# Value sums ordered behind the newest one-hots, the dense picks as a background task, score tiles in other PSUM banks and row norms one head later, in an encoder layer with expert retrieval

## The chip, the cores and the metric

One core of a Trainium2 chip. The metric is the device time of one execution in microseconds. Before the change three runs gave a median of 1346.87 us (1346.04 to 1347.17). The engines are PE (TensorE), DVE (VectorE), ACT (ScalarE), POOL (GpSimd) and SP (SyncE, which here only issues transfers). Every engine works off its own list of instructions in order.

## The reference

One encoder layer is applied to two sequences of 256 tokens, width 1024, each with 16 learned meta tokens in front: the *prompt* (s = 0) and the *sample* (s = 1). After a mixer (short gated convolution beside grouped-query attention) comes a retrieval over 128 x 128 = 16384 experts:

```python
q = (xf @ wq).reshape(T, 8, 2, 128)                  # 8 heads, two halves
s = einsum('thpc,hpnc->thpn', q, subkeys)            # 128 key scores per half
sv, si = top_k(s, 16)                                # 16 keys of each half
cv, cp = top_k(all 256 sums of the two halves, 16)   # 16 of the pairs
eidx = expert numbers;  gates = softmax(cv)
a = gelu(einsum('thkd,td->thk', u_tab[eidx], x)) * gates
out = einsum('thk,thkd->td', a, v_tab[eidx])         # 128 experts per token
```

Everything is float32.

## The kernel before, in words

**Two ways through the experts.** The prompt's experts are fetched: its 2 x 128 tokens have 128 experts each, and one transfer (`g_issue`, L178, on POOL's queue) brings for one rank `k` the rows `u` and `v` of the chosen expert of 128 tokens, 128 x 8 KB = 1.0486 MB, into a tile `grow`. There are 256 such transfers and four buffers for them. For each, DVE forms the dot product with the token (`g_dot`, L208, tile `grow`, result into `dots`), ACT applies gelu and the gate to `dots` (`g_weight`, L200 and L202), and DVE adds the weighted `v` row to the output row `xh` (`g_val`, L191: the *value sum*). Only then is the buffer free for the next transfer. The sample's experts are computed densely: scores of all 16384 experts in 128 *score blocks* `j` (a 512 KB load `u`, then matmuls `pSj`, L136, which the profile records 16 times a block), four blocks to a PSUM tile, evacuated with gelu by `experts` into `Al` and `Ah`; gates for all experts, mostly zero; and values in 128 blocks (`acc`, L1046) over 64 loads `v` of 1 MB. Every third value block is split into a high and a low part (`vhl`, `ah`, `al`).

**The order of the stages** in the trace: mixer of the prompt to 134 us, its retrieval projections to 190, mixer of the sample to 334, its projections (`projections`, matmuls `pqq`, key scores `pn`, L383) to 404, scores to 914, values to the end.

**The gates.** `gates_dense` runs beside the scores. After the picks are finished (`fin1`) it makes, in 64 steps of four tokens, one-hot tiles `oi` and `oj` on DVE, weighted copies `gh` and `gl` of `oj` on ACT, and products `pgm` on PE (`gate_products`, L919 and L920); every second step the products are copied into `Al` and `Ah` (ACT, blocks whose scores are not yet out) or multiplied into them (DVE, the others). Its small tiles lie in the pool `og`, which is closed when it ends; the first `v` tiles are then laid in that space.

**What paces the background.** Inside the loops `bg(us)` is called with the PE time of the piece just written, 3.5 for a score block, and pays two accounts: `credit["a"]` by `share["a"]`, of which each gather step costs `GU` = 2.65, and `credit["b"]` by `share["b"]`, of which the tasks (generators that yield their cost) are paid. Without a task `a` gets the sum of both shares, at most `SMAX`. In the stage of the sample's projections `step1` makes the picks of a head at once, inside the loop, and puts gather steps between them by `SR`. From block 3 on the shares are `SS` = 0.72 and `SBS` = 0.42. What is left of the 256 transfers at the values stage is spread over its blocks by `want`, each transfer waiting for the matmul of its block (`pe_mark`).

**Who sets the order.** The program writes instructions in the order of the Python code, and the tile framework's scheduler then reorders them on each engine within their dependencies. `order(i, before)` ties an instruction behind another of the same engine in that order, with no wait of its own. Before, each dot and each value sum is tied to the newest DVE instruction written at that moment (L190 to L192, L207 to L210).

**The row norms.** The sample's tokens `xr` enter the projections unscaled. `rescale` (L868) makes, at head 0, a PSUM tile `pb` of the row norms (`pb`, L877), and DVE multiplies it into the eight chunks of `xr` (L881); the key scores of the head projected before that are scaled in their evacuation (`hp < 2`).

**PSUM at the scores.** `psS`, two tiles of two banks for the scores, is opened before `psg`, two tiles for key scores and gate products; `acc` later takes the space of `psg`.

Of the kernel before, what the change touches and what calls it, by code (L numbers as in the profile page):

```python
# [37 lines left out]
SR = 0.6  # L38
SS = 0.72
SMAX = 0.74  # L40
SPL = 3
SBS = 0.42
# [3 lines left out]
def encoder_layer(ctx: ExitStack, tc: tile.TileContext, xp, xs_, meta, vec, w_in, w_out, wq,  # L46
# [23 lines left out]
    act = Recorded(nc.scalar, last_act)  # L70

# [3 lines left out]
    def ps(name, bufs):  # L75
        return tc.tile_pool(name=name, bufs=bufs, space=PSUM, reuse_waits="tile")
# [35 lines left out]
    def weights(src, s, split=False):  # L112

        w = [wtile("w").rearrange("p (c n) -> p c n", c=4) for _ in range(2)]
        for q in range(2):
            nc.sync.dma_start(w[q], src[:, s, 4 * q:4 * q + 4])
        if not split:
            return lambda c, k=0: w[c // 4][:, c % 4]
        k = 1 + 2 * spl[0]
        spl[0] = 1 - spl[0]  # L120
        hl = [ga[k + i].tile([P, 2 * D], F32R, tag="g", name=n).rearrange("p (q x) -> p q x", q=2)
              for i, n in enumerate(("whi", "wlo"))]
        for q in range(2):
            f = w[q].rearrange("p c n -> p (c n)")
            act.activation(hl[0][:, q], f, AF.Copy)
            dve.tensor_tensor(hl[1][:, q], f, hl[0][:, q].bitcast(F32), op=ALU.subtract)
        v = [x.rearrange("p q (c n) -> p (q c) n", c=4) for x in hl]
        return lambda c, k=0: v[k][:, c]
# [54 lines left out]
    def order(i, before):  # L183
        tc.add_manual_dep(i.ins, before.ins.name,
                          mybir.DependencyInfo(mybir.DependencyClass.NoSync, mybir.DependencyReason.DATA),
                          reason="order")

    def g_val():
        t, k, r = vals.pop(0)
        before = last[0]  # L190
        i = dve.scalar_tensor_tensor(gctx["h"], r[:, D:], dots[:, k:k + 1], gctx["h"], op0=ALU.mult, op1=ALU.add)  # L191
        order(i, before)  # L192
        if t == 0 and k == P - 1:
            pool.dma_start(yp[0:P, :], gctx["h"])
            gctx["h"] = gctx["next"][1]
# [19 lines left out]
    direct = [False]  # L215

# [158 lines left out]
    def projections(xr, sk, scores, qp, step=None, split=False, rescale=None, lag=1):  # L375
# [4 lines left out]
        def key_scores(hp, qs, pl=None, tag="tr"):  # L380
# [3 lines left out]
            if hp < 2 and rn is not None:  # L384
                for t in range(2):
                    act.activation(scores[:, hp, t], pn[:, t], AF.Copy, scale=rn[:, t:t + 1])
            else:
                act.activation(scores[:, hp], pn, AF.Copy)
# [3 lines left out]
        for hd in range(PH):  # L392
            w = weights(wq, hd, split)
            for pp in range(2):
# [7 lines left out]
                if hd == 0 and rescale is not None:  # L402
                    rn = rescale(xr, pp)
# [25 lines left out]
    w_kv = weights(w_in, 0, True)  # L429
# [39 lines left out]
    def front(s, h, rn):  # L469
# [17 lines left out]
        for t in range(2):  # L487
# [5 lines left out]
            if sp:  # L493
                dve.tensor_scalar_mul(x, h[:, t, :], stat)
            else:
                act.activation(x, h[:, t, :], AF.Copy, scale=stat)
# [363 lines left out]
    def step1(hd):  # L860
        share["a"] = 0.0
        for us in heads1(hd, [0, 1]):
            more(us * SR)
        topk_left[0] -= 1
# [3 lines left out]
    def rescale(xr, pp):  # L868

        if pp == 0:  # L870
# [13 lines left out]
    share.update(a=SR, b=0.0)  # L884
# [3 lines left out]
    psS = ctx.enter_context(ps("psS", 2))  # L888
    psgx = ExitStack()
    psg = psgx.enter_context(ps("psg", 2))  # L890
    r_done = [0]
    tau = [0]

    def gates_dense():
# [5 lines left out]
        yield 6.0  # L900
# [35 lines left out]
        for t in range(2):  # L936
# [15 lines left out]
            yield 3.0  # L952
            for o in range(P // OC):
# [7 lines left out]
                dve.tensor_tensor(v4(oi), sl4(0), ib, op=ALU.is_equal)  # L961
# [7 lines left out]
                if o == 0:  # L969
                    yield 2.0  # L970
                yield 1.3 + (4 * r_done[0] + 60) / 700
# [18 lines left out]
    for j in range(P):  # L990
# [12 lines left out]
        if j == 3:  # L1003
            tasks.append(gates_dense())
            share.update(a=SS, b=SBS)
# [124 lines left out]
```

## Time and profile before

| | us |
|---|---|
| median of 3 runs | 1346.87 |
| the profiled execution | 1346.99 |
| its span in the trace | 1345.2 |
| PE busy | 1275.6 (95%) |
| DVE busy | 1056.0 (78%) |
| transferred | 459.68 MB, mean 342 GB/s |
| value sums, 256 on DVE | 1282 ns each |
| dots, 256 on DVE | 1221 ns each |
| one-hots, `oi` or `oj` | 420 ns each |

The profiled execution lies 1.8 us above its span (what is outside of the first and last instruction). An idle time in the trace's timeline stands in brackets with what ended it. The granted clock is the share of full speed that TensorE had in a stretch. A DMA busy share of 1.00 means that all 16 DMA engines were busy throughout.

### The profile page before, as it was taken

The numbers are of one execution on the slowest core, as the hardware profiler recorded it, in microseconds if no ns is written. First come the engines' busy times: TensorE is split into PE (matmuls) and PEld (weight loads), VectorE is DVE, ScalarE is ACT, GpSimd is POOL, SyncE is SP. The second block draws the span as 40 slices with busy tenths as digits, with TensorE's granted clock in tenths as the row PEclk, the third lists the DMA queues.
The fourth block names the chain that finished last, engine by engine and source line by source line (L and its number), as shares of the span: only waits on it lengthen the run. The fifth ranks groups of instructions, "written<-read, shape, count | busy, mean of one in ns | idle before, by whom it ended". The sixth has DMA issues, their size and how long they took to land.

```text
span 1345.2 us, 17868 instructions
## 1 busy us (share of the span) xinstructions
PE 1275.6 (95%) x6038; PEld 965.0 (72%) x6038; DVE 1056.0 (78%) x2279; ACT 549.9 (41%) x1621; POOL 389.1 (29%) x480
## 2 busy tenths in 40 slices
PE   6999998998898999969999999996999999999998
PEld 5888996777787887758888888884555555555554
DVE  5656998885799998679888787897677777777767
ACT  5555641742221311148776555663222222222221
POOL 1111223431223343543233232231222232222221
PEclk9999998998999999989999999997999999999999
DMA  5534636658998999999999999997999999999997
GB/s 174 160 108 152 214 106 219 216 192 317 365 333 309 383 417 415 416 412 386 399 396 399 397 415 354 409 403 275 410 420 422 421 420 415 420 420 418 415 422 324
DMA packets 80859, 459.68 MB, mean 342 GB/s; under 512 B 9456, under 2 KB 9968, under 8 KB 39552
## 3 DMA queue, kind: packets, MB, share of 16 engines
q0 software_dynamic: 37296, 270.02, 50.1%
q1 hardware_dynamic: 42032, 183.57, 35.9%
q10 hardware_dynamic: 1440, 4.95, 1.0%
q8 instruction: 47, 0.77, 0.2%
q14 instruction: 44, 0.36, 0.1%
HBM read 454.28 MB, written 4.19 MB: 341 GB/s over the span
## 4 chain that ended last, share of the span: by engine, by line
PE 37%; DMA 17%; DVE 7%; issue 3%; ACT 2%; POOL 0%; DVEq 0%; POOLq 0%; ACTq 0%; SPq 0%
PE acc L1046 27%; DMA grow<-in_uv,eidx 16%; PE pSj L136 9%; DVE xh L63 3%; DVE grow L63 2%; DMA v<-in_v_n 1%; DVE Ah L63 1%; ACT dots L63 1%; DVE Al L63 1%; PE pgm L920 1%; PE pgm L919 1%; ACT gh L63 0%; ACT pSj L63 0%; DVE vhl L63 0%; ACT gl L63 0%
## 5 line engine op out<-in xcount | busy, mean ns | idle before, releaser
L178 POOL DMA_INDIRECT grow<-in_uv,eidx x256 | 317.2, 1239 | 717.2 <-DVE xh L63 233.5
L136 PE MATMUL pSj<-xr,u 128*128 128x256 f32 x2048 | 468.9, 386 | 7.4 <-ACT Ah L63 4.7
L136 PEld LDWEIGHTS pSj<-xr,u 128*128 128x128 f32 x2048 | 386.2, 192 | 69.0 <-DMA u<-in_u_t 7.5
L63 DVE SCALAR_TENSOR_TENSOR xh<-grow,dots,xh 128x1024 f32<-128x1024 f32 x256 | 328.2, 1282 | 58.4 <-ACT dots L63 57.2
L63 DVE SCALAR_TENSOR_TENSOR grow<-grow,xh 128x1024 f32<-128x1024 f32 x256 | 312.5, 1221 | 70.2 <-DMA grow<-in_uv,eidx 69.2
L63 ACT ACTIVATE dots<-dots 128x1 f32<-128x1 f32 x256 | 51.7, 202 | 544.8 <-DVE grow L63 544.4
L1046 PE MATMUL acc<-v,Al 128*128 128x512 f32 x496 | 220.1, 597 | 5.1 <-DMA v<-in_v_n 5.1
L1046 PEld LDWEIGHTS acc<-v,Al 128*128 128x128 f32 x496 | 94.9, 191 | 113.0 <-issue 110.5
L1046 PE MATMUL acc<-vhl,ah 128*128 128x512 f32 x336 | 107.4, 441 | 0.0
L63 ACT ACTIVATE gh<-oj,ghi 128x128 f16<-128x128 f16 x256 | 99.5, 389 | 6.2 <-PE pgm L919 5.7
L63 ACT ACTIVATE gl<-oj,glo 128x128 f16<-128x128 f16 x256 | 99.5, 389 | 0.0
L63 DVE TENSOR_TENSOR vhl<-v,vhl 128x1024 fp32r<-128x1024 f32 x42 | 51.4, 1224 | 55.6 <-ACT vhl L63 55.6
L1046 PEld LDWEIGHTS acc<-vhl,ah 128*128 128x128 f32 x336 | 63.2, 188 | 30.2 <-issue 19.1
L1046 PE MATMUL acc<-v,Ah 128*128 128x512 f32 x192 | 84.3, 592 | 0.0
L63 ACT ACTIVATE dots<-dots,gate_all 128x1 f32<-128x1 f32 x256 | 74.6, 292 | 7.0
L63 DVE TENSOR_TENSOR wlo<-w,whi 128x1024 fp32r<-128x1024 f32 x42 | 51.1, 1218 | 19.6 <-ACT whi L63 13.4
L1046 PEld LDWEIGHTS acc<-v,Ah 128*128 128x128 f32 x192 | 36.4, 190 | 41.2 <-issue 40.2
L136 PE MATMUL pqq<-xr,w 128*128 128x256 f32 x256 | 60.0, 388 | 0.8 <-DMA w<-in_wq 0.8
L136 PEld LDWEIGHTS pqq<-xr,w 128*128 128x128 f32 x256 | 48.6, 195 | 8.1 <-DMA w<-in_wq 1.4
L919 PE MATMUL pgm<-gh,oi 128*128 128x128 f16 x256 | 36.8, 222 | 16.1 <-DVE oi L63 15.1
L63 ACT ACTIVATE vhl<-v 128x1024 fp32r<-128x1024 f32 x42 | 44.0, 1048 | 19.1 <-DMA v<-in_v_n 18.4
L63 ACT ACTIVATE whi<-w 128x1024 fp32r<-128x1024 f32 x42 | 43.9, 1058 | 18.3 <-PE pqq L136 8.5
(279 smaller groups left out, 1753.6 us busy)
## 6 DMA issues: line engine op xcount, KB each, us to landing
u<-in_u_t SPq DMA_DIRECT2D x128, 512.0 KB, 8.6
v<-in_v_n SPq DMA_DIRECT2D x64, 1024.0 KB, 8.9
w<-in_w_in SPq DMA_DIRECT2D x36, 512.0 KB, 3.9
w<-in_wq SPq DMA_DIRECT2D x32, 512.0 KB, 6.1
w<-in_w_out SPq DMA_DIRECT2D x16, 512.0 KB, 4.7
grow<-in_uv,eidx POOLq DMA_INDIRECT x256, 10.1
hdram<-h ACTq DMA_DIRECT2D x3, 512.0 KB, 2.7
h<-in_xp SPq DMA_DIRECT2D x2, 512.0 KB, 5.9
```

Source lines behind the costliest of these rows:

```text
L63: i = f(*a, **k)
L136: i = pe.matmul(out, st_(c, a), mv(c, b), start=(n == 0), stop=(n == NC * len(terms) - 1))
L178: i = pool.indirect_dma_start(out=r, out_offset=None, in_=uv, in_offset=bass.IndirectOffsetOnAxis(ap=eidx[:, t, k:k + 1], axis=0))
L919: pe.matmul(pg[:, q, :], oi[:, r, :], gh[:, r, :], start=True, stop=False)
L920: pe.matmul(pg[:, q, :], oi[:, r, :], gl[:, r, :], start=False, stop=True)
L1046: i = pe.matmul(acc[t][q], a[:, t * P:(t + 1) * P], v[:, q * 512:(q + 1) * 512], start=j == 0 and n == 0, stop=j == P - 1 and n == len(ter ...
```

## The change

The picks of the sample become a background task, paid by `SRB` = 0.58 in the projections (`SR` is 0.57 instead of 0.6); the shares of the scores' stage, now `SSG` = 0.75 and `SBS` = 0.46, are set when the first one-hots are due and no longer at block 3, and `SMAX` goes from 0.74 to 0.66. A value sum is tied behind the newest `oi`. The row norms are multiplied into `xr` after the second head, so key scores of two heads are scaled in their evacuation. `psg` is opened before `psS`. The first weights' low parts (`wlo`) are ordered behind the first normalized tile (`xs`).

```diff
-SR = 0.6
-SS = 0.72
-SMAX = 0.74
+SR = 0.57
+SRB = 0.58
+SSG = 0.75
+SMAX = 0.66
-SBS = 0.42
+SBS = 0.46
...
+        def convert(behind=None):
+            for q in range(2):
+                f = w[q].rearrange("p c n -> p (c n)")
+                act.activation(hl[0][:, q], f, AF.Copy)
+                i = dve.tensor_tensor(hl[1][:, q], f, hl[0][:, q].bitcast(F32), op=ALU.subtract)
+                if behind is not None:
+                    order(i, behind)
...
         order(i, before)
+        if last_oi[0] is not None:
+            order(i, last_oi[0])
...
-            if hp < 2 and rn is not None:
+            if hp < 4 and rn is not None:
...
-                if hd == 0 and rescale is not None:
-                    rn = rescale(xr, pp)
+                if hd < 2 and pp and rescale is not None:
+                    rn = rescale(xr, hd)
...
-    w_kv = weights(w_in, 0, True)
+    convert_kv, w_kv = weights(w_in, 0, True, True)
...
-                dve.tensor_scalar_mul(x, h[:, t, :], stat)
+                i = dve.tensor_scalar_mul(x, h[:, t, :], stat)
+                if t == 0:
+                    convert_kv(i)
...
     def step1(hd):
-        share["a"] = 0.0
-        for us in heads1(hd, [0, 1]):
-            more(us * SR)
-        topk_left[0] -= 1
+        tasks.append(heads1(hd, [0, 1]))
...
-    share.update(a=SR, b=0.0)
+    share.update(a=SR, b=SRB)
...
-    psS = ctx.enter_context(ps("psS", 2))
     psgx = ExitStack()
     psg = psgx.enter_context(ps("psg", 2))
+    psS = psgx.enter_context(ps("psS", 2))
...
-        yield 6.0
+        yield 3.0
...
             yield 3.0
+            share.update(a=SSG, b=SBS)
             for o in range(P // OC):
...
-                dve.tensor_tensor(v4(oi), sl4(0), ib, op=ALU.is_equal)
+                last_oi[0] = dve.tensor_tensor(v4(oi), sl4(0), ib, op=ALU.is_equal)
...
-                if o == 0:
-                    yield 2.0
-                yield 1.3 + (4 * r_done[0] + 60) / 700
+                yield 1.2 + (4 * r_done[0] + 60) / 760
...
         if j == 3:
             tasks.append(gates_dense())
-            share.update(a=SS, b=SBS)
```

Three places where the order of instructions moves.

On DVE at the row norms of the sample (`grow` written: a dot; `xh` written: a value sum; the numbers are tile names), before:

```order
L63 SCALAR_TENSOR_TENSOR xh_1601<-grow_3453,dots_96,xh_1601 128x1024
L63 TENSOR_TENSOR xr_3347<-pb_3678,xr_3347 128x256 x8
L63 SCALAR_TENSOR_TENSOR grow_3543,dots_96<-grow_3543,xh_1601 128x1024
L63 SCALAR_TENSOR_TENSOR xh_1601<-grow_3482,dots_96,xh_1601 128x1024
L63 SCALAR_TENSOR_TENSOR xh_1601<-grow_3514,dots_96,xh_1601 128x1024
L63 SCALAR_TENSOR_TENSOR grow_3584,dots_96<-grow_3584,xh_1601 128x1024
L63 SCALAR_TENSOR_TENSOR xh_1601<-grow_3543,dots_96,xh_1601 128x1024
```

and now:

```order
L64 SCALAR_TENSOR_TENSOR xh_1601<-grow_3453,dots_96,xh_1601 128x1024
L64 SCALAR_TENSOR_TENSOR xh_1601<-grow_3482,dots_96,xh_1601 128x1024
L64 SCALAR_TENSOR_TENSOR grow_3543,dots_96<-grow_3543,xh_1601 128x1024
L64 SCALAR_TENSOR_TENSOR xh_1601<-grow_3514,dots_96,xh_1601 128x1024
L64 SCALAR_TENSOR_TENSOR grow_3584,dots_96<-grow_3584,xh_1601 128x1024
L64 SCALAR_TENSOR_TENSOR xh_1601<-grow_3543,dots_96,xh_1601 128x1024
L64 TENSOR_TENSOR xr_3347<-pb_3695,xr_3347 128x256 x8
```

The eight multiplications into `xr` move behind three value sums and two dots, the second of these on the transfer `grow_3584`.

On DVE at the first one-hots, before:

```order
L63 TENSOR_TENSOR oj_5363<-dup_5165,io_5154 128x512
L63 SCALAR_TENSOR_TENSOR xh_1601<-grow_5102,dots_96,xh_1601 128x1024
L63 SCALAR_TENSOR_TENSOR grow_5118,dots_96<-grow_5118,xh_1601 128x1024
L63 SCALAR_TENSOR_TENSOR xh_1601<-grow_5118,dots_96,xh_1601 128x1024
L63 SCALAR_TENSOR_TENSOR grow_5134,dots_96<-grow_5134,xh_1601 128x1024
L63 SCALAR_TENSOR_TENSOR xh_1601<-grow_5134,dots_96,xh_1601 128x1024
L63 SCALAR_TENSOR_TENSOR grow_5183,dots_96<-grow_5183,xh_1601 128x1024
L63 SCALAR_TENSOR_TENSOR xh_1601<-grow_5183,dots_96,xh_1601 128x1024
L63 TENSOR_TENSOR oi_5317<-dup_5165,io_5154 128x512
```

and now:

```order
L64 TENSOR_TENSOR oi_5264<-dup_5231,io_5220 128x512
L64 TENSOR_TENSOR oj_5265<-dup_5231,io_5220 128x512
L64 SCALAR_TENSOR_TENSOR xh_1601<-grow_5153,dots_96,xh_1601 128x1024
L64 SCALAR_TENSOR_TENSOR grow_5184,dots_96<-grow_5184,xh_1601 128x1024
L64 TENSOR_TENSOR oi_5296<-dup_5231,io_5220 128x512
L64 TENSOR_TENSOR oj_5297<-dup_5231,io_5220 128x512
L64 SCALAR_TENSOR_TENSOR xh_1601<-grow_5184,dots_96,xh_1601 128x1024
L64 SCALAR_TENSOR_TENSOR grow_5202,dots_96<-grow_5202,xh_1601 128x1024
L64 TENSOR_TENSOR oj_5336<-dup_5231,io_5220 128x512
L64 TENSOR_TENSOR oj_5377<-dup_5231,io_5220 128x512
L64 TENSOR_TENSOR oi_5335<-dup_5231,io_5220 128x512
```

Four value sums and three dots stood between one `oj` and the next `oi`; now at most one of each stands there.

On PE at the end of the scores (`pgm`: gate products, `pSj`: scores, `acc`: values), before:

```order
L919 LDWEIGHTS oi_8142
L919 MATMUL pgm_8156<-gh_8144,oi_8142 128x128
L920 LDWEIGHTS oi_8142
L920 MATMUL pgm_8156<-gl_8145,oi_8142 128x128
L1046 MATMUL acc0_0_8187<-v_8192,Al_3651 128x512
L1046 MATMUL acc0_1_8188<-v_8192,Al_3651 128x512
L1046 MATMUL acc1_0_8189<-v_8192,Al_3651 128x512
L1046 MATMUL acc1_1_8190<-v_8192,Al_3651 128x512
```

and now:

```order
L929 LDWEIGHTS oi_7972
L929 MATMUL pgm_7986<-gh_7974,oi_7972 128x128
L930 LDWEIGHTS oi_7972
L930 MATMUL pgm_7986<-gl_7975,oi_7972 128x128
L149 MATMUL pSj_7919<-xr_3347,u_8029 128x256 x8
L149 MATMUL pSj_8041<-xr_3347,u_8039 128x256 x8
L149 MATMUL pSj_8041<-xr_3347,u_8058 128x256 x8
L149 MATMUL pSj_8041<-xr_3347,u_8074 128x256 x8
L149 MATMUL pSj_8041<-xr_3347,u_8090 128x256 x8
L1054 MATMUL acc0_0_8120<-v_8125,Al_3651 128x512
L1054 MATMUL acc0_1_8121<-v_8125,Al_3651 128x512
```

The last gate products stood behind all scores, directly ahead of the first values; now five score blocks stand between.

## Rows read from the trace of the kernel before

**Rows 1.** The page: its first line, and the chain of work that ended last, by engine.
```profile
span 1345.2 us, 17868 instructions
...
PE 37%; DMA 17%; DVE 7%; issue 3%; ACT 2%; POOL 0%; DVEq 0%; POOLq 0%; ACTq 0%; SPq 0%
```

**Rows 2.** The table of stretches over the dense part of the program (microseconds from the span's start): length; busy us of PE, of its weight load, of DVE, ACT and POOL, each with its count of records; then the granted TensorE clock, the mean busy share of the 16 DMA engines, and GB/s. The last line is of the same view, one stretch of 10 us alone.
```profile
409.00:442.00 33.00, 33.00 (x150) 28.82 (x150) 33.00 (x176) 4.71 (x14) 14.13 (x33) 0.96 0.88 321
442.00:578.00 136.00, 133.82 (x595) 110.28 (x594) 113.52 (x185) 32.57 (x92) 55.90 (x37) 1.00 1.01 409
578.00:612.00 34.00, 22.65 (x105) 17.86 (x104) 27.60 (x41) 18.39 (x63) 15.40 (x10) 0.80 1.00 393
612.00:816.00 204.00, 204.00 (x1170) 178.09 (x1169) 168.85 (x266) 140.77 (x484) 63.43 (x54) 1.00 1.00 400
...
914.00:946.00 32.00, 21.47 (x70) 11.33 (x68) 19.55 (x27) 8.69 (x26) 6.13 (x5) 0.79 0.76 288
946.00:1326.00 380.00, 379.34 (x1105) 208.46 (x1104) 282.28 (x355) 96.63 (x263) 108.31 (x93) 1.00 1.01 420
1326.00:1346.00 20.00, 15.10 (x41) 7.38 (x39) 12.20 (x16) 2.75 (x8) 0.00 (x0) 0.94 0.61 243
...
1220.00:1230.00 10.00, 10.00 (x30) 5.49 (x29) 7.11 (x9) 2.36 (x6) 2.14 (x3) 1.00 1.02 425
```

**Rows 3.** The timeline of PE with scores alone (first line) and in the steady part of the one-hot steps: start, us, engine, line, operation, tiles, count.
```profile
441.80 10.52 PE L136 MATMUL pSj<-xr,u 128*128 128x256 f32 x48
...
641.40 0.22 PE L919 MATMUL pgm<-gh,oi 128*128 128x128 f16 x1
...
641.85 3.67 PE L136 MATMUL pSj<-xr,u 128*128 128x256 f32 x16
```

**Rows 4.** The timeline of PE in the values stage: the first matmuls of two successive split blocks.
```profile
1272.92 1.48 PE L1046 MATMUL acc<-vhl,ah 128*128 128x512 f32 x4
...
1282.54 1.48 PE L1046 MATMUL acc<-vhl,ah 128*128 128x512 f32 x4
```

**Rows 5.** The table of waits in the values stage, 946 to 1326 us: who waited for whom, us in total, times, the longest.
```profile
POOL grow L178 <- PE acc L1046: 159.7, 51, 5.2
```

**Rows 6.** The DMA view from 914 us to the end: packets and bytes.
```profile
DMA packets 24456, 173.56 MB, mean 402 GB/s; under 512 B 2704, under 2 KB 2704, under 8 KB 3600
```

**Rows 7.** The timeline at the start: PE's first work, and DVE's last step ahead of it.
```profile
12.65 0.69 PE L461 MATMUL pt<-ident,xs 128*128 128x128 f32 x2 [12.65 <-DVE ss L63]
...
11.85 0.75 DVE L63 TENSOR_SCALAR xs<-h,stat 128x1024 f32<-128x1024 f32 x1
```

**Rows 8.** The timeline around the row norms of the sample (DVE, then POOL, then PE).
```profile
342.58 1.28 DVE L63 SCALAR_TENSOR_TENSOR xh<-grow,dots,xh 128x1024 f32<-128x1024 f32 x1 [1.45 <-ACT dots L63]
343.78 1.41 DVE L63 TENSOR_TENSOR xr<-pb,xr 128x256 f32<-128x256 f32 x4
...
355.09 1.23 DVE L63 SCALAR_TENSOR_TENSOR grow<-grow,xh 128x1024 f32<-128x1024 f32 x1 [3.39 <-DMA grow<-in_uv,eidx]
...
344.64 1.00 POOL L178 DMA_INDIRECT grow<-in_uv,eidx  x1 [2.54 <-DVE xr L63]
...
343.49 10.91 PE L136 MATMUL pqq<-xr,w 128*128 128x256 f32 x42
...
355.02 3.26 PE L136 MATMUL pqq<-xr,w 128*128 128x256 f32 x14 [0.18 <-DMA w<-in_wq]
```

**Rows 9.** The timeline of PE at the first score block.
```profile
402.56 1.28 PE L383 MATMUL pn<-Ah,qs 128*128 128x128 f32 x10
408.57 8.77 PE L136 MATMUL pSj<-xr,u 128*128 128x256 f32 x32 [4.74 <-ACT Ah L63]
```

**Rows 10.** The DMA view of 442 to 578 us: loads of `u`, KB each, and the median time from issue to landing.
```profile
u<-in_u_t SPq DMA_DIRECT2D x37, 512.0 KB, 11.2
```

**Rows 11.** The timeline around the first one-hots (PE, then DVE).
```profile
588.73 3.72 PE L136 MATMUL pSj<-xr,u 128*128 128x256 f32 x16 [0.50 <-ACT Al L63]
602.03 0.29 PE L919 MATMUL pgm<-gh,oi 128*128 128x128 f16 x1 [9.58 <-DVE oi L63]
...
603.75 6.67 PE L136 MATMUL pSj<-xr,u 128*128 128x256 f32 x16
...
589.21 1.28 DVE L63 SCALAR_TENSOR_TENSOR xh<-grow,dots,xh 128x1024 f32<-128x1024 f32 x1 [0.26 <-ACT dots L63]
591.13 1.23 DVE L63 SCALAR_TENSOR_TENSOR grow<-grow,xh 128x1024 f32<-128x1024 f32 x1 [0.64 <-DMA grow<-in_uv,eidx]
...
601.55 0.42 DVE L63 TENSOR_TENSOR oi<-dup,io 128x512 f16<-128x512 f16 x1
```

**Rows 12.** The value sums among the groups of DVE instructions in 612 to 816 us: names, shape, count | busy us, mean ns | idle time before them and what ended it.
```profile
L63 DVE SCALAR_TENSOR_TENSOR xh<-grow,dots,xh 128x1024 f32<-128x1024 f32 x50 | 64.0, 1281 | 6.0 <-ACT dots L63 5.3
```

**Rows 13.** The timeline at the change from scores to values (PE, SyncE's queue, POOL).
```profile
910.13 3.67 PE L136 MATMUL pSj<-xr,u 128*128 128x256 f32 x16
...
920.17 0.29 PE L919 MATMUL pgm<-gh,oi 128*128 128x128 f16 x1 [5.47 <-DVE oi L63]
...
926.26 4.57 PE L1046 MATMUL acc<-v,Al 128*128 128x512 f32 x5 [5.05 <-DMA v<-in_v_n]
...
921.27 1.80 SPq L1026 DMA_DIRECT2D v<-in_v_n  x3
...
935.82 1.29 POOL L178 DMA_INDIRECT grow<-in_uv,eidx  x1 [17.50 <-PE acc L1046]
```

More of the change, by code (lines that the diff above doesn't have):

```diff
@@ L70, in encoder_layer, with order @@
     act = Recorded(nc.scalar, last_act)
+    def order(i, before):
+        tc.add_manual_dep(i.ins, before.ins.name,
+                          mybir.DependencyInfo(mybir.DependencyClass.NoSync, mybir.DependencyReason.DATA),
+                          reason="order")
     def sb(name, bufs, side="left"):
@@ L110, in wtile, with weights @@
         return wp.tile([P, D], F32, tag="w", name=name)
-    def weights(src, s, split=False):
+    def weights(src, s, split=False, late=False):
         w = [wtile("w").rearrange("p (c n) -> p c n", c=4) for _ in range(2)]
@@ L122, in weights @@
               for i, n in enumerate(("whi", "wlo"))]
[L123 to L126, printed above, removed]
+        def convert(behind=None):
[5 more added lines that the diff above has]
+                    order(i, behind)
         v = [x.rearrange("p q (c n) -> p (q c) n", c=4) for x in hl]
+        if late:
+            return convert, lambda c, k=0: v[k][:, c]
+        convert()
         return lambda c, k=0: v[k][:, c]
@@ L181, in g_issue @@
         pend.append((t, k, r))
[L183 to L186, printed above, removed]
     def g_val():
@@ L215, in encoder_layer @@
     direct = [False]
+    last_oi = [None]
     def gather(n=1):
@@ L860, in step1, with rescale @@
     def step1(hd):
-        share["a"] = 0.0
-        for us in heads1(hd, [0, 1]):
-            more(us * SR)
-        topk_left[0] -= 1
+        tasks.append(heads1(hd, [0, 1]))
     rows = []
-    def rescale(xr, pp):
-        if pp == 0:
+    def rescale(xr, hd):
+        if hd == 0:
             on = q1.tile([P, P], F32, name="on", bufs=1)
```

## The prediction, on record before the change was run

> **What bounds the kernel now.** I read the chain that ended last first: PE 37%, DMA 17%, DVE 7% [rows 1]. One resource does not bind throughout, so the second view is the table of stretches [rows 2]. Read PE's busy time against the length, the granted clock, and GB/s. In 612 to 816 us PE is busy throughout and full. In 442 to 578 it is not (133.8 of 136), while the DMA engines are busy without a gap at 409 GB/s. In 578 to 612 PE stands for 11 us, and the granted clock is 0.80, a mix of the two levels 2.4 and 1.2 GHz. In 914 to 946 PE stands for 10.5 us and the transfers fall to 288 GB/s. In 946 to 1326 both are full: PE 379.3 of 380, DMA at a share of 1.01 and 420 GB/s.
>
> Prices of undisturbed work come third, from timelines. A score block is 16 records; 48 in a row take 10.52 us, 16 by themselves 3.67, and the last record's lap over the next instruction belongs to no block, which leaves about 3.44 us a block [rows 3]. The gate products of a one-hot step take 0.45, from 641.40 to 641.85. So 128 blocks and 64 steps cost 128 x 3.44 + 64 x 0.45 = 469 us, and the dense stage takes 914 - 404 = 510. Some 40 us are lost there, and the change touches the places of most of them. Three value blocks take 9.62 us [rows 4], so 128 take 410 us.
>
> **The parts and their costs.** The sum is made against the profiled execution (1346.99 us, 1.8 above its span of 1345.2; it lies 0.1 above the median of the runs). Negative is a gain.
>
> *Start.* PE's first work follows the end of the chain on DVE, `xs` at 11.85 [rows 7]. The low parts of the weights, of which one lies directly ahead of it there (1.22 us), go behind. `xs` can come 1.2 us or a little more sooner, but the first product also wants a low part, which now comes later. I take -1.5; bounds 0 and -2.5 (two such parts).
>
> *Row norms.* DVE now works the eight multiplications into `xr` behind the dot of a transfer that POOL issues at 344.64, as a value sum has freed its buffer at 343.86; it lands at 355.1 [rows 8]. Then come the dot (1.23 us) and a value sum (1.28), so `xr` starts near 357.7. Head 2 needs it. In the trace PE does heads 0 and 1 from 343.49 to about 354.2, and head 2 starts at 355.02, waiting for its weights. So head 2 is late by 3 us. Who waits behind: all of PE's list, since the next key scores need little. I take +3. Ends: +6, if after the idle time PE also gets the lower clock; -3.5, if DVE reaches `xr` early and the wait of 3.5 us that PE had for `pb` before 343 disappears.
>
> *First score block.* PE ends its key scores at 403.84 and starts the scores at 408.57, after 4.74 us for an ACT copy of key scores; its first 32 records then take 8.77 us [rows 9] where two blocks cost 7.1 (3.67 + 3.44). That is 4.7 + 1.7 = 6.4 us. The copy itself lasts 0.37 us: it stands in ACT's list behind gelus that wait for DVE's dots. The score tiles now lie in the banks of the projections' products, whose copies are long done. Key scores that are left go between the first score blocks. I take -5.4 (one short wait remains); bounds -6.4 and 0.
>
> *Loads of `u`.* In 442 to 578 PE has 595 records, 127.9 us at 3.44 per 16: 8 us are lost. With 0.72 x 3.5 / 2.65 = 0.95 transfers per block the demand is (0.95 x 1.049 + 0.524) MB in 3.44 us = 442 GB/s, above the 409 that flowed; `u` takes 11.2 us to land [rows 10]. Until the one-hots begin the share is now 0.57, 0.75 transfers and 381 GB/s. I take -7; bounds -8 and 0.
>
> *First one-hots.* PE stands 9.58 us up to 602.03 for an `oi` and 0.50 ahead of the block before, 0.7 more behind it, and the next 16 records take 6.67 instead of 3.67 us. On DVE the `oi` came behind four rounds of value sum and dot, each some 3.75 us from one dot to the next (589.21, 591.13 and onwards to 601.55), waiting in every round for ACT and for a transfer [rows 11]. Idle 10.8 and clock 3.5 (with the slow gate products) make 14.3 us. In the new order one round at most stands there. It can cost 3 us once. I take -11.5; bounds -14.3 and -4 (two rounds remain in the way).
>
> *The rest of the dense stage.* PE is full in 612 to 816 [rows 2]. One thing is new: a value sum behind the newest one-hot keeps its buffer longer, and the next transfer comes later. With 0.99 transfers per block (share 0.75) and fewer blocks under it, the one-hots are denser too: steps over 71 blocks where 80 had them. DVE's busy share, 0.83, becomes about 0.92. I take 0; bounds -3 (the small stalls of 816 to 850 go) and +10.
>
> *Values stage.* This is what has to be paid. By the pacing rules worked through for both kernels, 157 dots lie ahead of the first value block before and 146 now: less share up to the one-hots. So 110 transfers are left instead of 99, 11.5 MB more. After 914 us 173.6 MB flow [rows 6]. At 420 GB/s that is 413.2 us of the 431.2 up to the end, and the other 18 are two holes [rows 2]: 914 to 946 moves 9.2 MB, 21.9 us at full rate, so 10.1 lost; the end, likewise, 7.6. The first hole has its cause in [rows 13]: the last gate products wait 5.47 us for an `oi`, `v` is issued only at 921.27 because it is laid over the space of the one-hots, `acc` starts at 926.26, and POOL's next transfer waits 17.5 us for `acc`. Now the last gate products stand five score blocks ahead, so `v` can be there when scores end, and `acc` takes the banks of `psg`, free by then. I leave 3 us of that hole. About 1 MB of `v` lands earlier. So 173.6 + 11.5 - 1 = 184.1 MB. PE would allow 410 + about 5 us, which needs 444 GB/s; the best 10 us of the stage show 425 [rows 2]. So transfers bind and PE waits for `v`. POOL had time to wait for PE, 159.7 us in 51 waits [rows 5], so there is room to ask for more, and I take 422.5, between the stage's mean and its best. 184.1 / 0.4225 = 435.7, + 7.6 + 3 = 446.3 against 431.2: **+15**. Bounds: +9.6 at 425 without the hole; +27 at 420 with the whole hole and no early `v`.
>
> The Trainium skill (DMA: Bandwidth & Descriptors, Specifications) gives some 358 GB/s as one core's share of HBM and 435 as the ceiling of the fabric. The trace's 420 over 380 us is above the first and below the second, so only the second could matter; by it, an estimate, the stage would cost +3 instead of +15.
>
> Sum: -1.5 + 3 - 5.4 - 7 - 11.5 + 0 + 15 = **-7.4**, 1339.6 us. Its own range, with the terms half-way to their bounds, is 1332 to 1346.
>
> **Rivals.**
>
> *A, slower: DVE becomes the pace of the one-hot steps.* Tied behind the newest one-hot, each value sum also holds all behind it on DVE: the next one-hots and the products into `Al`, for which PE's next step waits. If each of the 64 steps is late by one wait for ACT like the 0.60 us between dot and value sum, that is 38 us, 1378. It passes no change at 7.4 / 64 = 0.12 us per step. Against it: a value sum waits 5.3 us over 50 now [rows 12], and DVE has 17% free. For it: DVE is the fullest engine after PE there.
>
> *B, not faster: the values stage pays in full.* The +27 in place of +15, all else as forecast: 1351.6. For it: 420 is the rate at a share of 1.01, with transfers always waiting. Against: the order on PE shows the gate products moved away.
>
> *C, the change does not do what it says.* The order of instructions is no time. If DVE is behind by the same rounds when the first one-hots are due, PE stands there as before: -7.4 + 11.5 = +4.1, 1351.1.
>
> *D, much faster.* The transfers have no ceiling at 425, or the later rate brings more of them forward than I count, as the shorter dense stage (-24 by the terms) suggests: the values stage costs +3, row norms nothing, 1347.0 - 7.4 - 12 - 3 = 1324.6. Against: no 10 us show it.
>
> **How the numbers follow.** About 0.2%, 2.7 us, is what a measurement of this kernel tells from no change. Chances: forecast 0.49, D 0.14, B 0.14, C 0.10, A 0.13. The forecast's own range is faster by over 2.7 us in nine cases of ten and else within; D is faster; B and C are slower by about 4.5, in 4 of 10 cases nearer than 2.7; A is slower in all but a mild form. Faster: 0.44 + 0.14 + 0.04 = 0.62. Same: 0.05 + 0.09 + 0.01 = 0.15. Slower: 0.23. The range reaches down to D and up beyond B and C: 1324 to 1356; outside are most of A and the tails of D.
>
> **What would show it.** In the profile after: no wait of PE over 4 us for `oi` in the scores; the first `pSj` directly behind the key scores; PE busy over 0.99 in the stretch before the one-hots, at about 380 GB/s; `xr` multiplied behind 357 and PE idle there for some 3 us; scores ending near 890 and `acc` within 3 us of it; a values stage of 435 to 450 us at 420 to 425 GB/s, with PE waiting for `v`, 110 transfers in it. The forecast is wrong if PE waits for one-hots again and again (A), if the dense stage is no shorter by 15 us (C), or if the values stage moves over 430 GB/s or has clearly fewer transfers left (D).

## The result and the profile after

The changed kernel takes 1355.76 us (median of 4 runs, 1354.14 to 1358.09), the kernel before on the same chip 1346.70 (1346.04 to 1347.17): ratio 1.0069, interval 1.0050 to 1.0088. It is slower by 9 us. The profiled execution has a span of 1352.4 us against 1345.2 [rows 1], so 7.2 of them can be looked for in the trace.

The table of stretches of the changed kernel, to be read against [rows 2] (length; busy us of PE, PE's weight load, DVE, ACT, POOL; granted clock, DMA share, GB/s):

```profile
442.00:578.00 136.00, 127.38 (x581) 111.36 (x581) 112.19 (x263) 30.52 (x79) 44.05 (x46) 0.96 0.94 368
578.00:612.00 34.00, 34.00 (x179) 29.77 (x178) 17.85 (x30) 15.66 (x51) 7.37 (x7) 1.00 0.98 379
612.00:816.00 204.00, 203.22 (x1209) 177.08 (x1207) 181.37 (x292) 158.68 (x550) 61.21 (x53) 1.00 1.00 395
914.00:946.00 32.00, 30.02 (x86) 15.56 (x85) 24.29 (x31) 7.74 (x22) 9.45 (x9) 1.00 1.01 419
946.00:1326.00 380.00, 361.89 (x1022) 192.81 (x1020) 287.00 (x360) 93.20 (x265) 114.27 (x96) 0.99 1.01 415
```

Two holes are gone: PE is full in 578 to 612, and 914 to 946 moves 419 GB/s instead of 288. But in 442 to 578 the transfers fall from 409 to 368 GB/s, 5.6 MB less, and PE still does not get through more blocks (36 loads of `u` against 37). In the values stage PE is busy for 362 of 380 us, where it was busy for 379, while the DMA share is 1.01.

PE's timeline of the changed kernel, from the row norms to the first value block:

```profile
357.03 3.35 PE L149 MATMUL pqq<-xr,w 128*128 128x256 f32 x7 [4.57 <-DVE xr L64]
...
405.57 3.62 PE L149 MATMUL pSj<-xr,u 128*128 128x256 f32 x16
...
436.75 3.51 PE L149 MATMUL pSj<-xr,u 128*128 128x256 f32 x15 [2.05 <-ACT Al L64]
...
487.08 13.19 PE L149 MATMUL pSj<-xr,u 128*128 128x256 f32 x51 [8.62 <-ACT Al L64]
...
603.34 0.22 PE L929 MATMUL pgm<-gh,oi 128*128 128x128 f16 x1
...
856.41 0.29 PE L929 MATMUL pgm<-gh,oi 128*128 128x128 f16 x1 [5.43 <-DVE oi L64]
...
902.94 7.11 PE L1054 MATMUL acc<-v,Al 128*128 128x512 f32 x16
```

The wait for `xr` is as forecast [rows 8], the scores start without a wait [rows 9], the first one-hots come in time [rows 11], and the values start right behind the scores [rows 13]. New are the waits for ACT at 436 and 487 and for an `oi` at 856. What ACT did ahead of the second:

```profile
472.93 0.31 ACT L64 ACTIVATE gate_all<-gate_all 128x128 f32<-128x128 f32 x1 [5.71 <-DVE gate_all L64]
...
480.10 0.20 ACT L64 ACTIVATE dots<-dots 128x1 f32<-128x1 f32 x1 [3.85 <-DVE grow L64]
...
484.38 0.31 ACT L64 ACTIVATE gate_all<-gate_all 128x128 f32<-128x128 f32 x1 [2.45 <-DVE gate_all L64]
484.71 1.28 ACT L64 ACT_TABLE_LOAD   x1
486.00 1.02 ACT L64 ACTIVATE Al<-pSj 128x1024 f32<-128x1024 f32 x1
```

The evacuation of the scores (`Al<-pSj`) stands in ACT's list behind two exponentials of the sample's gates and behind gelus of dots, and each of these waits for DVE, which is still making the picks or finishing them. The picks run 23 us later than before: their last MAX8 and index searches end at 473 instead of 450. And on POOL:

```profile
454.01 2.94 POOL L303 TENSOR_TENSOR cd<-Al 128x32 f32<-128x32 f32 x5 [7.97 <-DVE Al L64]
...
457.43 0.95 POOL L191 DMA_INDIRECT grow<-in_uv,eidx  x1
458.69 1.33 POOL L191 DMA_INDIRECT grow<-in_uv,eidx  x1 [0.31 <-issue]
469.96 0.90 POOL L303 TENSOR_TENSOR cd<-Al 128x32 f32<-128x32 f32 x5 [9.95 <-DVE Al L64]
...
471.34 0.96 POOL L191 DMA_INDIRECT grow<-in_uv,eidx  x1
472.61 1.10 POOL L191 DMA_INDIRECT grow<-in_uv,eidx  x1 [0.30 <-issue]
```

The pair sums of the picks (`cd`) wait for DVE, and two transfers behind them go out together the moment they are done: they had their buffers and stood in line. In 466 to 476 us 257 GB/s flow, where 419 flowed before.

### The profile page after: what moved, and what is told of

It reads as the page before. It is cut to its first block, busy times and chain, and to the rows that moved or that the text cites. A ratio compares the mean times of both kernels' runs of the same rounds, so it can differ in the third digit from the quotient of the medians.

```text
span 1352.4 us, 17884 instructions
## 1 busy us (share of the span) xinstructions
PE 1274.4 (94%) x6038; PEld 964.9 (71%) x6038; DVE 1054.3 (78%) x2276; ACT 549.9 (41%) x1622; POOL 388.3 (29%) x480
## 2 busy tenths in 40 slices
DMA packets 80859, 459.68 MB, mean 340 GB/s; under 512 B 9456, under 2 KB 9968, under 8 KB 39552
## 4 chain that ended last, share of the span: by engine, by line
PE 23%; DMA 18%; DVE 15%; issue 7%; ACT 5%; POOL 0%; DVEq 0%; POOLq 0%; ACTq 0%
PE pSj L149 18%; DMA grow<-in_uv,eidx 18%; DVE xh L64 7%; PE acc L1054 4%; DVE grow L64 3%; ACT dots L64 2%; DVE Al L64 2%; DVE vhl L64 2%; ACT vhl L64 1%; DMA v<-in_v_n 1%; PE pgm L929 0%; PE pgm L930 0%; DVE al L64 0%; ACT gh L64 0%; ACT Al L64 0%
## 5 line engine op out<-in xcount | busy, mean ns | idle before, releaser
L191 POOL DMA_INDIRECT grow<-in_uv,eidx x256 | 308.1, 1204 | 713.7 <-DVE xh L64 204.3
L149 PE MATMUL pSj<-xr,u 128*128 128x256 f32 x2048 | 460.9, 383 | 10.7 <-ACT Al L64 10.7
L149 PEld LDWEIGHTS pSj<-xr,u 128*128 128x128 f32 x2048 | 385.8, 191 | 61.4 <-ACT Al L64 11.5
L1054 PE MATMUL acc<-vhl,al 128*128 128x512 f32 x168 | 49.8, 420 | 19.0 <-DVE al L64 18.4
L1054 PEld LDWEIGHTS acc<-vhl,al 128*128 128x128 f32 x168 | 30.2, 193 | 35.2 <-DVE al L64 30.0
```

What stands on the lines that cost most here:

```text
L149: i = pe.matmul(out, st_(c, a), mv(c, b), start=(n == 0), stop=(n == NC * len(terms) - 1))
L191: i = pool.indirect_dma_start(out=r, out_offset=None, in_=uv, in_offset=bass.IndirectOffsetOnAxis(ap=eidx[:, t, k:k + 1], axis=0))
L1054: i = pe.matmul(acc[t][q], a[:, t * P:(t + 1) * P], v[:, q * 512:(q + 1) * 512], start=j == 0 and n == 0, stop=j == P - 1 and n == len(ter ...
```

## The ledger of bytes

All these programs move 459.68 MB, and from 442 us on the queues are nearly always full. So I added up GB/s by length from the table of stretches, cut at the same points in every kernel: MB moved up to that point less those of the kernel before. The last columns are what the lag at 1300 us makes at 420 GB/s, and the span measured against 1345.2.

| kernel | at 442 | 578 | 900 | 950 | 1300 | us | span |
|---|---|---|---|---|---|---|---|
| changed | +0.1 | -5.5 | -6.8 | -1.3 | -3.2 | +7.6 | +7.2 |
| rows_undone | -0.1 | -4.7 | -5.9 | -0.8 | -1.9 | +4.5 | +4.1 |
| pacing_undone | -2.2 | -2.0 | -0.9 | -0.4 | -1.6 | +3.8 | +4.3 |
| late_in_before | +0.8 | +0.8 | -2.2 | -0.5 | -0.8 | +1.9 | +1.4 |
| more_early | 0.0 | -1.9 | -2.0 | +3.4 | +3.3 | -7.9 | -8.5 |
| sums_on_dve | +0.1 | -3.3 | -4.5 | +0.8 | -2.0 | +4.8 | +5.0 |
| sums_and_exps | 0.0 | -3.0 | -3.8 | +1.4 | -0.4 | +1.0 | +2.2 |
| picks_at_once | +1.1 | -0.4 | -2.2 | +2.9 | +3.0 | -7.1 | -7.4 |
| onehots_alone | -2.6 | -2.5 | -3.9 | +1.6 | -0.6 | +1.4 | +3.2 |

The last two columns must agree, since every kernel moves the same total and what is left at 1300 goes at much the same rate. What the ledger tells is where a lag arises. The changed kernel loses 5.6 MB between 442 and 578, 1.3 more up to 900, gains 5.5 (13 us) between 900 and 950, where the hole was, and loses 1.9 again in the values stage, at 415 GB/s.

## The experiments

Ratios are to the kernel before on the same chip. The chips of the experiments scatter more than the first: the kernel before spread over 1338 to 1354 us there, with medians of 1342.85 to 1345.78 where the first chip had 1346.70. Single profiles differ by some us in the front too, as the column at 442 shows, and a profiled execution can lie 7.5 us off the median of its kernel (tie_undone: 1354.77 and 1362.28). So a span that differs by some us from that of another chip shows no gain by itself.

**Parts put back one at a time.**

```diff
 # pacing_undone: the changed kernel with
-        tasks.append(heads1(hd, [0, 1]))
+        share["a"] = 0.0
+        for us in heads1(hd, [0, 1]):
+            more(us * SR)
+        topk_left[0] -= 1
 # and SR, SS, SMAX, SBS and the yields of before
```

> The changed kernel with its whole pacing put back (picks at once inside the projections, the old shares, SMAX, and yields); the tie, the banks, the row norms and the start stay as changed. Theory 1 (the pacing costs: the picks' gate exponentials hold up ACT's evacuation of the scores, 11 us, and 11 transfers more lie in the values stage, 18 us; the tie and the banks gain): before 1346.7 less 5 for the banks, plus 2.6 for the row norms, less about 10 for the first one-hots: 1334, and 157 dots ahead of the values. Theory 2 (the tie costs: buffers held longer, so that transfers and then one-hots come late): 1346 to 1352.

Measured: 1.0024 (0.9997 to 1.0052), span 1349.5. The first theory misses; the time lies in the range of the second, but by luck, for the next run shows that the tie does nothing. It does not remove the first wait for an `oi`, which is there as before:

```profile
607.36 0.29 PE L932 MATMUL pgm<-gh,oi 128*128 128x128 f16 x1 [9.57 <-DVE oi L64]
```

```diff
 # tie_undone
-        if last_oi[0] is not None:
-            order(i, last_oi[0])
```

> The changed kernel without the tie of value sums behind the newest oi. Theory 1: the wait of PE for the first oi comes back, some 10 us, and the 8.6 us wait near 480 us stays: 1364. Theory 2: faster than the changed kernel, 1346 to 1350, and the 5.4 us wait of PE for oi near 856 us is gone.

Measured: 1.0139 (1.0090 to 1.0188), span 1353.0, waits of 8.50 and 5.05 us in the same two places, none at the first one-hots. The order of instructions is the same as the changed kernel's on every engine, line for line. So the tie does nothing here: the 1364 of the first theory is nearly met, but without its wait. The two ratios of what is one program, 1.0069 and 1.0139, tell how far apart two chips put it. This program (median 1362.28) is also what the other parts put back are to be compared with, for they ran on its chip: pacing_undone has 1348.83 there, rows_undone 1350.90, banks_undone 1360.52.

```diff
 # rows_undone
-            if hp < 4 and rn is not None:
+            if hp < 2 and rn is not None:
-                if hd < 2 and pp and rescale is not None:
-                    rn = rescale(xr, hd)
+                if hd == 0 and rescale is not None:
+                    rn = rescale(xr, pp)
```

> The changed kernel with the row norms multiplied in at head 0 again. Theory 1: PE's 4.6 us wait for xr at 357 us goes, another of 3.5 for pb comes; the first score block starts 2.5 us sooner and the end with it: 1353. Rival (what the front gains is eaten by later waits for transfers): 1355 to 1356, no change.

Measured: 1.0039 (1.0010 to 1.0068), span 1349.3. The scores start at 401.09 instead of 405.57. The wait of 8.6 us for ACT also became two of 3.6 and 3.1 (at 437 and 540). The gain of 3.1 us of span is what was expected; on its own chip the gain is 11 us, and no run here says why it is so much more.

```diff
 # banks_undone
+    psS = ctx.enter_context(ps("psS", 2))
     psgx = ExitStack()
     psg = psgx.enter_context(ps("psg", 2))
-    psS = psgx.enter_context(ps("psS", 2))
```

> The changed kernel with psS opened before psg again. Theory 1: PE waits some 4 us ahead of the first score block, then at half clock: 1361. Rival (eaten later by waits for transfers): 1356.

Measured: 1.0119 (1.0074 to 1.0164), span 1352.4, that of the changed kernel. The scores start at 405.51, 0.95 us behind the projections' end, so the 1361 is met without the wait that it was to come from. The wait that I gave to the banks goes with the picks' new place alone, and in picks_at_once below, which has the new banks, it comes back one block later.

**What the values stage is bound by.**

```diff
 # fewer_transfers
-        queue.extend((1, k) for k in range(P))
+        queue.extend((1, k) for k in range(P - 11))
 # eleven_unread: UNREAD = range(22, 123, 10)
-            if pend:
+            if pend and pend[0][0] == 1 and pend[0][1] in UNREAD:
+                pend.pop(0)
+            elif pend:
                 g_dot()
 # more_early: the changed kernel; late_in_before: the kernel before
+            share.update(a=0.72)                  # more_early, at j == 3
+            share.update(a=0.57, b=SBS)           # late_in_before, at j == 3,
+            share.update(a=SS, b=SBS)             # and at the first one-hots
```

> The changed kernel without the last 11 ranks of the prompt's second tile: 99 transfers are left for the values stage, with their dots and value sums gone too. If transfers bind there, 11 x 1.0486 MB at 0.42 go: 27 us less in the values stage, but no further than PE's own pace of some 415 us: span about 1325. If the values stage is bound by something else (DVE's split of every third block), 0 to 10 us less.

> The changed kernel; 11 of the 110 transfers of the values stage arrive, but their dot, gate and value sum are left out (27 us of DVE). If transfers bind: no change, within 4 us, since the bytes are the same. If DVE's list binds (the split al behind dots and sums): 15 to 27 us less.

> The changed kernel with share a = 0.72 from block 3 up to the first one-hots (where it has 0.57): 155 dots ahead of the values instead of 146, so 101 transfers left. Theory 1: the values stage is 9 x 1.0486 / 0.42 = 22 us shorter, the stage of the loads of u loses up to 8 us: some 14 us less than the changed kernel. Rival (the bytes are only moved, and the dense stage is full of transfers as well): no change.

> The kernel before with one number changed: share a = 0.57 from block 3 to the first one-hots, 0.72 again from there. 149 dots ahead of the values, 107 transfers left instead of 99. Ledger of bytes: 442 to 578 us falls from 409 to some 370 GB/s, 5 MB or 13 us, which come at the end: ratio 1.008 to 1.011, as the whole change. Rival (PE gains the 8 us of the loads of u and the hole at 930 us takes up the rest): ratio 0.999 to 1.003.

| kernel | transfers left | worked on by DVE | first to last `acc`, us | span | ratio |
|---|---|---|---|---|---|
| before | 99 | 99 | 414.8 | 1345.2 | |
| changed | 110 | 110 | 444.5 | 1352.4 | 1.0069 (1.0050 to 1.0088) |
| fewer_transfers | 99 | 99 | 415.5 | 1323.9 | 0.9880 (0.9845 to 0.9915) |
| eleven_unread | 110 | 99 | 448.0 | 1360.6 | 1.0099 (1.0059 to 1.0139) |
| more_early | 101 | 101 | 419.0 | 1336.7 | 0.9992 (0.9970 to 1.0013) |
| late_in_before | 107 | 107 | 433.4 | 1346.6 | 1.0046 (1.0020 to 1.0072) |

With 11 transfers fewer the stage is 29 us shorter. With all transfers and 27 us less of DVE's work it is not shorter at all. The waits of PE for `al` in it, up to 2.75 us each, look like DVE's fault and are not: `al` stands in DVE's list behind dots that wait for transfers, and 11.5 MB at 420 GB/s are 27 us. The longest of them in the changed kernel (DVE, then PE):

```profile
1280.97 1.22 DVE L64 SCALAR_TENSOR_TENSOR grow<-grow,xh 128x1024 f32<-128x1024 f32 x1 [1.83 <-DMA grow<-in_uv,eidx]
...
1285.26 1.23 DVE L64 SCALAR_TENSOR_TENSOR grow<-grow,xh 128x1024 f32<-128x1024 f32 x1 [1.18 <-DMA grow<-in_uv,eidx]
...
1287.55 0.42 DVE L64 TENSOR_TENSOR al<-Ah,ah 128x256 fp32r<-128x256 f32 x1
...
1288.03 1.21 PE L1054 MATMUL acc<-vhl,al 128*128 128x512 f32 x4 [2.75 <-DVE al L64]
```

So transfers bind here, as the forecast had it. `more_early` undoes the lower share alone in the changed kernel, and the whole loss goes: 15.7 us of span, where 14 were expected, and 1.0069 becomes 0.9992. `late_in_before` shows that the lower share alone costs: about +0.46%, between its two expectations, and less than the 0.8 to 1.1% of the first, since 442 to 578 stays at 409 GB/s there. In the changed kernel the same share moves 368. Something else takes transfers away in that stretch.

**What takes them away.**

```diff
 # gates_first
-            yield from fin1(t)
+            gates1(t)             # of both tiles, then decode1(t) of both
 # exps_left_out
-            act.activation(gate_all[...], gate_all[...], AF.Exp, ...)
+            if t0 == 0: ...       # the prompt's only
 # picks_at_once: step1 of before, and at j == 3
+            share.update(a=SR, b=0.42)
 # sums_on_dve (sums_and_exps: with exps_left_out)
+            pool = dve if t0 == 2 else nc.gpsimd   # in pairs_top
```

> The changed kernel with one edit: the gates (subtract, exponential, normalize) of both sample tiles are made ahead of both decodes. Theory 1 (ACT's second gate exponential waits for DVE, which does the first tile's decode, and score evacuation stands behind it): PE's 8.6 us wait for ACT near 480 us falls to under 3 us, scores end some 6 to 9 us sooner, and the end by less than that if transfers bind the values stage. Rival (it is ACT's table loads or the general lag of DVE): the wait stays over 6 us.

Measured, on the rival's side: the wait falls to 6.38 us only, with others of 2.84 (at 441 us) and 1.41 (at 549); 1.0079 (1.0043 to 1.0116). The two exponentials go out together, and the evacuation still waits behind gelus for DVE.

> The changed kernel without the two exponentials on the sample's gates (and so without the table loads around them). If ACT's evacuation is held up by these alone: no wait of PE for ACT over 3 us near 480. If it is the gelus of the dots, which wait for a DVE full of picks: a wait of 3 us or more stays there.

Measured: a wait of 2.12 us in place of 8.62, span 1348.1 (one execution). The exponentials make most of it:

```profile
482.49 14.08 PE L149 MATMUL pSj<-xr,u 128*128 128x256 f32 x64 [2.12 <-ACT Al L64]
```

> The changed kernel with the picks of a head made at once in the projections again; shares 0.6 there, 0.57 and 0.42 from block 3, then 0.75 and 0.46 as in the change. Theory 1 (the waits of PE for ACT's evacuation at 437 and 487 us come from the picks pushed into the scores): both under 2 us; a wait of some 4 us ahead of the first score block comes back; 106 transfers left; span some 5 to 10 under the changed kernel's 1352. Rival (they come from the gates' exponentials, which any order has): a wait of over 5 us stays near 450 to 490.

Measured: no wait for ACT over 1 us up to 520, then 4.35 at 522; a wait of 3.46 for a copy of key scores at 404; span 1337.8, ratio 0.9985 (0.9965 to 1.0005). The first theory has the waits right, and the time falls further than it said. `SR` was 0.57 in this run and not the 0.6 of the expectation, and the wait for an `oi` behind the start of the second tile is there as well, 5.80 us at 840.

> The changed kernel with the pair sums of the sample's picks (tile cd) on DVE instead of POOL, so that they no longer stand ahead of transfers in POOL's list. If the holds of 8.0 and 10.0 us there cost the transfers of 456 to 496 us: 442 to 578 us moves 375 GB/s or more instead of 368, span 3 to 6 under the changed kernel's 1352.4. If pace and order set the rate and the holds only shift transfers: 365 to 370 GB/s, and the span within 2 us or longer by the work added to DVE.

> The changed kernel with the pair sums on DVE and without the two exponentials on the sample's gates: neither POOL nor ACT waits for the picks in the scores. If both waits together make the loss of 442 to 578 us: 390 GB/s or more there and a span of 1343 to 1346. If the lower share does: not over 380 GB/s, 1348.

The stretch of 442 to 578 us, in the columns of the table of stretches, in late_in_before, picks_at_once, sums_on_dve and sums_and_exps:

```profile
442.00:578.00 136.00, 133.85 (x607) 111.86 (x606) 111.49 (x182) 37.17 (x106) 48.51 (x36) 1.00 1.01 409
442.00:578.00 136.00, 129.41 (x612) 111.57 (x611) 113.30 (x192) 45.55 (x135) 50.86 (x40) 0.99 1.00 398
442.00:578.00 136.00, 132.26 (x602) 114.74 (x601) 118.35 (x307) 30.60 (x79) 35.16 (x30) 0.99 0.96 384
442.00:578.00 136.00, 135.04 (x621) 117.05 (x619) 120.15 (x315) 25.33 (x76) 42.85 (x31) 1.00 0.98 387
```

Measured for sums_on_dve: 384 GB/s, and PE's wait for ACT falls to 3.66 us; span 1350.2, but a ratio of 1.0068 (1.0048 to 1.0087), which is no gain. With both waits away (one execution of a kernel that leaves out the exponentials): 387 GB/s, PE all but full, 621 records instead of 581, span 1347.4. Neither of its two expectations is met: 387 is not 390, nor 380. By the profiles the waits account for 2.5 of the 5.6 MB in the stretch. What they cost in time is not shown: the span is 5 us under that of the changed kernel, but the kernel before is 3.9 us faster on this chip too (1342.85), and against it this execution (1349.12) is still 6.3 us slower.

**Combinations.**

```diff
 # onehots_alone: the kernel before with
-                if o == 0:
-                    yield 2.0
-                yield 1.3 + (4 * r_done[0] + 60) / 700
+                yield 1.2 + (4 * r_done[0] + 60) / 760
 # and share.update(a=0.75, b=0.46) ahead of the loop over o
 # early_and_rows: more_early with rows_undone; picks_early: picks_at_once with
-            share.update(a=SR, b=0.42)
+            share.update(a=0.68, b=0.42)
```

> The kernel before with one part of the change: no extra yield behind the first one-hots, the steps' yields 1.2 + (4 r + 60) / 760, and the shares 0.75 and 0.46 from the first one-hots on (0.72 and 0.42 until then, as before). By the order of instructions one value sum and one dot at most stand between the first one-hots, where four and three stood. Theory 1 (that place sets PE's wait of 9.6 us for the first oi, not the tie): the wait is under 3 us, the last gate products lie 14 blocks ahead of the values, and 96 transfers are left: 1325 to 1333. Rival (denser steps and more transfers overload DVE or the queues in the scores): new waits there, 1340 or more.

Measured: 0.9995 (0.9972 to 1.0019), span 1348.4; the rival's side. The wait for `oi` goes, so the yields with the shares beside them are enough for that, and so does the hole. But others come (the first stands ahead of all that the edit touches, where the kernel before waits 4.74 us [rows 9]):

```profile
414.41 5.92 PE L136 MATMUL pSj<-xr,u 128*128 128x256 f32 x13 [6.30 <-ACT Ah L63]
...
587.17 0.22 PE L919 MATMUL pgm<-gh,oi 128*128 128x128 f16 x1 [4.96 <-ACT gh L63]
...
831.27 0.29 PE L919 MATMUL pgm<-gh,oi 128*128 128x128 f16 x1 [6.61 <-ACT gl L63]
...
931.56 7.11 PE L1045 MATMUL acc<-v,Al 128*128 128x512 f32 x16 [1.34 <-DMA v<-in_v_n]
```

In late_in_before, with the yields of before, there is no wait at the first one-hots either; the lower share alone is enough too:

```profile
556.17 21.21 PE L136 MATMUL pSj<-xr,u 128*128 128x256 f32 x96
577.22 0.22 PE L919 MATMUL pgm<-gh,oi 128*128 128x128 f16 x1
```

> The changed kernel with two edits: share a = 0.72 from block 3 to the first one-hots, and the row norms at head 0 again. If the two gains add (more_early moved the span from 1352.4 to 1336.7, rows_undone to 1349.3): span 1331 to 1335. If the second is eaten by waits for transfers: 1336 to 1338.

Measured: 1.0020 (0.9991 to 1.0048), span 1345.4, outside of both expectations. The gains do not add.

> picks_at_once with share a = 0.68 instead of 0.57 from block 3 to the first one-hots: 155 dots ahead of the values instead of 150, 101 transfers left. By the ledger of transferred bytes (the end comes when 459.7 MB have gone, at some 420 GB/s from 442 us on): 442 to 578 us at 405 to 410 GB/s where picks_at_once had 398, span some 3 to 6 under its 1337.8, ratio to before 0.994 to 0.997. Rival (PE's waits for loads of u and for ACT come back): 0.998 to 1.002.

Measured: 1.0004 (0.9986 to 1.0022), span 1341.4: the rival. None of the versions that do all the work is faster than the kernel before by more than its interval; picks_at_once comes nearest.

**The same profiles, cut at the end of the scores.**

| kernel | transfers left | first to last `pSj`, us | from there to the end |
|---|---|---|---|
| before | 99 | 505.2 | 431.4 |
| changed | 110 | 497.5 | 449.3 |
| late_in_before | 107 | 489.3 | 452.0 |
| exps_left_out | 110 | 493.5 | 447.5 |
| sums_on_dve | 110 | 490.7 | 452.0 |
| sums_and_exps | 110 | 489.9 | 450.3 |
| picks_at_once | 106 | 505.7 | 434.6 |
| more_early | 101 | 506.9 | 424.1 |

Each row is one execution. Fewer transfers beside the scores make the scores shorter and what follows longer: by 15.9 and 20.6 us for the lower share alone. With 110 transfers left, the waits of the picks cost the scores up to 7.6 us (497.5 against 489.9). picks_at_once does not have shorter scores than the changed kernel: its gain lies behind them, with four transfers fewer left and 420 GB/s instead of 415.

## Why the prediction was wrong, step by step

It forecast 1339.6 and the kernel takes 1355.8. On the profile -7.4 stands against +7.2, and the 14.6 us between lie in two steps, 11.7 up to the end of the scores and 2.9 behind it.

- **Start, -1.5: nothing came.** PE's first work is at 7.30 instead of 12.65 [rows 7], but its first product waits for ACT until 11.94, and by 108 us the two kernels are 0.2 us apart.
- **Row norms, +3: right.** Head 2 starts 2.0 us later, the projections end 2.6 later; rows_undone gives it back.
- **First score block, -5.4: right in size, wrong in cause.** The scores start 3.0 us earlier in spite of the later projections. The banks were neither needed for it (banks_undone) nor enough (picks_at_once).
- **Loads of `u`, -7, and first one-hots, -11.5: the waits are gone.** For the loads the gain is seen only where the picks do not take it away again: 621 records in 442 to 578 in sums_and_exps against 595 before, 5.6 us; late_in_before has 607, 2.6 us. The first one-hots owe it to the pacing, of which the yields and the lower share are each enough, and not to the tie, which I had taken from the order of the changed kernel without asking which edit moved it.
- **The rest of the dense stage, 0 with bounds -3 and +10: this failed.** The forecast had the scores end 22.4 us sooner; they end 10.7 sooner (903.1 against 913.8). Of this, 3.9 were forecast ahead of the scores and 3.0 came; 18.5 were forecast from their start on and 7.7 came. So 10.8 us are missing there. The prediction's own sign, PE busy over 0.99 at about 380 GB/s ahead of the one-hots, reads 0.94 at 368. New waits of 2.05 and 8.62 us and 2.1 of half clock (51 records in 13.19 us where 11.1 would do) lie at 436 to 500, 5.43 and some 1.6 of half clock at 856 (the next block takes 4.86 instead of 3.67, the gate products twice their time). They come to 19.8, more than what is missing, since more went of the old waits than the 18.5 that were booked. The one at 856 stands just behind the start of the prompt's second tile, whose first dot is at 833. DVE waits 6.44 us for a transfer there, with an `oi` behind it:

```profile
844.50 0.44 DVE L64 TENSOR_TENSOR oj<-dup,io 128x512 f16<-128x512 f16 x1
851.38 1.22 DVE L64 SCALAR_TENSOR_TENSOR grow<-grow,xh 128x1024 f32<-128x1024 f32 x1 [6.44 <-DMA grow<-in_uv,eidx]
```

  The prediction costed the picks as a background task at nothing and did not name what they stand ahead of. They were moved ahead of score evacuations in ACT's list and of transfers in POOL's, and there they wait for DVE. With their waits away the scores are 7.6 us shorter (sums_and_exps), 18.5 would then be missed by 3.2, and the wait at 856 is still there. Where that one comes from stays open.
- **Values stage, +15: right in kind, 3 us short.** From the end of the scores it takes 449.3 us against 431.4, +17.9. 183.5 MB flow there (184.1 forecast) at a mean of 408 GB/s; the hole is gone altogether, but the 422.5 GB/s of the forecast do not come: where before had 420, it is 415. PE waits for `al`, not for `v`. Rival D's ceiling of 435 GB/s, which the Trainium skill gives (DMA: Bandwidth & Descriptors, Specifications), is reached by no stage here; the highest mean of one is 420, and 10 us of the changed kernel move 426.
- **The sum itself** added PE's time in the scores to bytes in the values as if they were separate accounts. The queues were full during the removed wait too, at 393 GB/s [rows 2], so it may have cost little. This is argued and not shown: onehots_alone takes that wait and the hole away without putting transfers off, and is no faster, but it has new waits of 4.96 and 6.61 us.

Of the rivals, B and C come nearest by number (1351.6 and 1351.1), B without its reason: no hole remained, and the values stage cost 17.9 and not 27. C's sign did come, a dense stage that is not shorter by 15 us, but not its reason, a wait at the first one-hots. A, one-hots late in every step, did not come, nor did D.

What stays open: how the 9 us of the timed runs divide between the lower share and the picks' waits. Timed, the lower share alone costs 0.46% in the kernel before, and either edit undone in the changed kernel, the share (0.9992) or the place of the picks (0.9985, with the lower share kept), takes back the whole 0.69%; so the two do not add. Of the picks' waits, those on POOL were taken away and timed (sums_on_dve), with no gain.

## What to carry to other kernels

Where the queues are full over most of the span, keep a ledger of bytes first, and count a removed wait of an engine only if more bytes flow for it. A task put into the background lands in the list of every engine that it uses: for each, name what stands behind it there (here score evacuations on ACT, transfers on POOL). And ask of each edit by itself whether it moves an instruction; one of the five moved none.

## What was not expected of the hardware

Removing 27 us of DVE work from a stage in which PE waits for DVE left its length as it was (448.0 against 444.5 us). A TensorE stall of 8.62 us was followed by 51 records at 13.19 instead of 11.1 us, at a granted clock of 0.74 to 0.75 in the 10-us stretches around it, a mix of 2.4 and 1.2 GHz. The same program measured 1.0069 and 1.0139 of the same kernel before on two chips.
